# A two-layer decoder trunk on one core: the remainders of the weight pieces are made by an adding transfer instead of a DVE subtraction

## Chip, cores and metric

The kernel runs on 1 core of one Trainium2 chip. The metric is the device time of one execution in microseconds (us). The kernel before takes 2521.07 us, the median of 3 runs (2515.82 to 2522.28).

## What is computed

```
for layer in range(DEPTH):                       # DEPTH = 2, SEQ = 1024, D_MODEL = 1024
    h = rms_norm(x, norm_mix[layer])
    proj = h @ w_in[layer]                       # 1024 x 3584
    q_a, k_a, v_a, q_h, f_h, i_h, g_h = jnp.split(proj, split_points, axis=-1)
    attn = dilated_attention_group(q_a, k_a, v_a, positions)     # 8 heads, 3 strided windows
    attn = rms_norm(attn, attn_out_gain[layer])
    rec = hgrn2_group(q_h, f_h, i_h, g_h, lower_bounds[layer], hgrn_out_gain[layer])
    mixed = jnp.concatenate([attn, rec], axis=-1).astype(x.dtype)
    x = x + mixed @ w_out[layer]                 # 1024 x 1024
    h = rms_norm(x, norm_mlp[layer])
    x = x + jnp.square(jax.nn.relu(h @ w_up[layer])) @ w_down[layer]   # 1024 x 4096 x 1024
return rms_norm(x, norm_final)
```

## The kernel before

Everything stands transposed, features on the 128 partitions and tokens along the free dimension, in two halves of 512 tokens. A float32 product is made of three fast ones: each operand is split into a rounded part (`hi`, type fp32r) and the remainder (`lo` = source - `hi`), and TensorE adds hi·hi, hi·lo and lo·hi into one PSUM bank (`gemm`, lines 376 to 378, and `gemm_tok`, 401 to 403, for products with tokens on the partitions).

Weights come in groups of 128 x 2048. A group is loaded by SP in two halves of 128 x 1024 (512 KB, tag `raw`, 4 buffers). Each half gives two pieces of 128 x 512. `parts` (line 359) makes the pair of one piece in two buffers, `whi` and `wlo` (8 of each): ACT rounds the piece (line 317), DVE subtracts (line 319). `Group.piece` calls it for the weights as loaded. `up_rest` calls it also for s1 to s4, sums and differences of weight pieces: the MLP's first product uses Strassen's scheme with 7 products for 8, of which 3 read pieces as loaded and 4 read s1 to s4. Names of pieces: w0u80l is layer 0, up projection, group 8, piece 0, the remainder. The letters are h (recurrent projections), a (attention projections), o (output projection), u (up), d (down).

A layer runs through: projections and recurrence of the four recurrent heads, attention projections and attention with the first part of the output projection woven in, the norm of the attention output with the rest of the output projection, the MLP's up projection (16 groups), and its down projection. At the very start, the input is scaled, squared and split by ACT and DVE (`norm_in`: `n_0h`, `n_0l`, `n00sq` for the first token half, `n_1h`, `n_1l`, `n01sq` for the second), the squares are summed by two matmuls (`n00ms`, `n01ms`) and the first projection (`psf`, then `psq`) uses the pieces w0h000 to w0h003, then w0h010 to w0h013.

The order of instructions on each engine is not the program's order. Every operation is entered with `op(engine, cost, writes, reads, emit)`, and `Program.order` (line 131) plays the whole program as a list schedule with those costs. Each engine takes the earliest entered operation that is ready and whose buffers are free, at most `LOOKAHEAD` of TensorE work ahead of the oldest one open. A result counts as ready `LATENCY` after its end on another engine, and a buffer as free `RELEASE` after its last reader's end. The order that comes out is then fixed: on the chip each engine goes through its list and waits where an operand isn't there.

Of the kernel before, what the change touches and what calls it, by code (L numbers as in the profile page):

```python
# [11 lines left out]
F32 = mybir.dt.float32  # L12
F32R = mybir.dt.float32r
U32 = mybir.dt.uint32
AF = mybir.ActivationFunctionType
OP = mybir.AluOpType
# [21 lines left out]

COUNT = {"kk": 3, "slot": 64, "raw": 4, "trig": 2, "whi": 8, "wlo": 8, "ls": 4, "last": 2, "row": 2, "rc": 4, "z": 2, "gemm": 3, "sc": 2, "tr": 2, "acc": 1,
         "dram": 1 << 20, "const": 1 << 20}  # L40
LOOKAHEAD = {"PE": 60e3, "SP": 36e3}
PATIENCE = 5e3
RELEASE = {"PE": 200.0, "ACT": 190.0, "DVE": 190.0, "SP": 900.0}
TABLES = {"ln": "natural_log_exp_and_others", "sig": "sigmoid_and_others"}


# [70 lines left out]
class Program:  # L117

    LATENCY = {"PE": 210.0, "ACT": 190.0, "DVE": 190.0, "SP": 1800.0}
    TABLE = 1280.0

    def __init__(self):
# [2 lines left out]
    def op(self, eng, cost, writes, reads, emit, table=None, join=False):  # L127
        engines = eng if isinstance(eng, dict) else {eng: cost}
        self.ops.append(Op(len(self.ops), engines, list(writes), list(reads), emit, table, join))

    def order(self):
        free = dict(COUNT)
        busy = {e: 0.0 for e in self.LATENCY}
        ready = {e: [] for e in self.LATENCY}
        table = "ln"
# [17 lines left out]
        def arrive(o):  # L153
            for e in o.engines:
                heapq.heappush(ready[e], (o.index, o))
# [8 lines left out]
        while done < len(self.ops):  # L164
            while oldest < len(self.ops) and self.ops[oldest].start is not None:
                oldest += 1
            for e in ready:
# [3 lines left out]
                while ready[e]:  # L171
                    item = heapq.heappop(ready[e])
                    o = item[1]
                    if o.start is not None:
                        continue
                    kept.append(item)
                    if oldest < len(self.ops) and ahead[o.index] > ahead[oldest] + LOOKAHEAD.get(e, 60e3):
                        break
# [27 lines left out]
                o = pick  # L206
# [17 lines left out]
            now, _, kind, o = heapq.heappop(events)  # L224
            if kind == "end":
                done += 1
                for b in o.bufs:
                    b.left -= 1
                    if not b.left:
                        seq += 1  # L230
                        heapq.heappush(events, (now + RELEASE[o.on], seq, "free", b))
                for s in o.succs:
                    lag = 0.0 if s.engines.keys() == {o.on} and o.on != "SP" else self.LATENCY[o.on]
                    s.ready = max(s.ready, now + lag)
                    s.waiting -= 1
                    if not s.waiting:
                        seq += 1
                        heapq.heappush(events, (max(now, s.ready), seq, "ready", s))
            elif kind == "free":
                free[o.tag] += 1  # L240
                held[o.tag][oldest:o.last + 1] -= 1
            elif kind == "ready":
                arrive(o)
# [5 lines left out]
def trunk(ctx: ExitStack, tc: tile.TileContext, xT, wts, cols, trig, toep, lmask, ident_d, out):  # L249
    nc = tc.nc  # L250
    V, A, PE = nc.vector, nc.scalar, nc.tensor
# [15 lines left out]
    op = prog.op  # L267
# [26 lines left out]
    def c_act(n):  # L294
        return 80.0 + 0.833 * n

    def c_tt(n):
        return 65.0 + 1.042 * n
# [9 lines left out]
    def whole(b):  # L308
        return b, lambda: b.t
# [5 lines left out]
    def split(hi, lo, src, n=W, join=False):  # L315

        op("ACT", c_act(n), [hi[0]], [src[0]], lambda e: A.copy(hi[1](), src[1]()), join=join)  # L317
        op("DVE", c_tt(n), [lo[0]], [src[0], hi[0]],
           lambda e: V.tensor_tensor(lo[1](), src[1](), hi[1]().bitcast(F32), op=OP.subtract), join=join)  # L319
# [20 lines left out]
    class Group:  # L340
# [13 lines left out]
        def piece(self, i):  # L354
            if i not in self.pieces:
                self.pieces[i] = parts(self.raw(i), f"{self.name}{i}")
            return self.pieces[i]

    def parts(src, name):
        hi, lo = Buf(name + "h", "whi", [128, 512], F32R), Buf(name + "l", "wlo", [128, 512], F32R)  # L360
        split(whole(hi), whole(lo), src, 512)
        return hi, lo

    def gemm(ps, pieces, xs, ts=slice(0, W)):
# [140 lines left out]
    def table():  # L505
        return [[None] * NH for _ in range(KT)]
# [64 lines left out]
    for l in range(L):  # L571
# [628 lines left out]
        hf32, xmid, scale = table(), table(), [None] * NH  # L1200
# [84 lines left out]
        def up_rest(j, grp):  # L1285
            m1 = m1s[j]
            a11, a12, a21, a22 = (grp.raw(i) for i in range(4))
            s1, s2, s3, s4 = (slot(f"s{i}") for i in range(4))
            u2, u3, c12, c22 = (slot(n) for n in ("u2", "u3", "c12", "c22"))
            tt(whole(s1), a21, a22, OP.add)  # L1290
            tt(whole(s2), whole(s1), a11, OP.subtract)
            p = product(parts(whole(s2), "s2"), "t2", "tr")
            tt(whole(u2), whole(m1), p, OP.add)
            tt(whole(s3), a11, a21, OP.subtract)
            p = product(parts(whole(s3), "s3"), "t3", "gemm")
            tt(whole(u3), whole(u2), p, OP.add)
            p = product(parts(whole(s1), "s1"), "t1", "sc")
            tt(whole(c22), whole(u3), p, OP.add)
            relu2(j, 1, 1, c22)
            tt(whole(c12), whole(u2), p, OP.add)  # L1300
            p = product(grp.piece(3), "t4", "tr")
            tt(whole(u3), whole(u3), p, OP.subtract)
            relu2(j, 1, 0, u3)
            tt(whole(s4), a12, whole(s2), OP.subtract)
            p = product(parts(whole(s4), "s4"), "22", "gemm")
            tt(whole(c12), whole(c12), p, OP.add)
            relu2(j, 0, 1, c12)
# [175 lines left out]
```

## Time and profile before

| | us |
|---|---|
| median of 3 runs | 2521.07 (2515.82 to 2522.28) |
| profiled execution, its own time | 2519.49 |
| its span, first to last instruction | 2517.7 |
| TensorE (PE) busy in the span | 2481.2 (99%) |
| weight loads of TensorE (PEld) | 2102.3 (84%) |
| DVE busy | 1685.0 (67%) |
| ACT busy | 966.5 (38%) |
| GpSimd (POOL) busy | 0.2, 4 instructions |
| packets of SP's DMA queue, share of the 16 DMA engines | 37.8%, 314.74 MB |

The profile is of one execution, whose own time lies 1.6 us below the median of the runs. Time outside of the span is 1.8 us. An instruction is named by its line in the kernel, its engine, and its output and inputs. PE's granted clock is 0.995 of full speed over the span. A PE that is busy throughout a stretch is the bound there, whatever the others do; where it is idle, the view of waits names what it waited for.

### The profile page before, as it was taken

How to read it: one execution, taken by the hardware profiler on the slowest of the kernel's cores; microseconds unless marked ns; L12 is line 12 of the kernel's file. 1: busy time of each engine (PE TensorE's matmuls, PEld its weight loads, DVE VectorE, ACT ScalarE, POOL GpSimd, SP SyncE). 2: the span in 40 equal slices, each digit the busy share in tenths (PEclk: the TensorE clock that was granted, in tenths of full speed). 3: DMA queues.
4: the chain of work that ended last, by engine and by line, in shares of the span. 5: the costliest groups of instructions: out<-in, count | busy, mean ns of one | idle time of the engine just before them, and what ended most of it. 6: DMA issues, size and time to landing. Idle time of an engine off the chain costs nothing.

```text
span 2517.7 us, 34893 instructions
## 1 busy us (share of the span) xinstructions
PE 2481.2 (99%) x13004; PEld 2102.3 (84%) x13004; DVE 1685.0 (67%) x3358; ACT 966.5 (38%) x1953; POOL 0.2 (0%) x4
## 2 busy tenths in 40 slices
PE   9999999999999999999999999999999999999998
PEld 7898889787888888888888989898788888888887
DVE  6366868789977675434744678687899777555356
ACT  7233347667322232121432334476662223222123
POOL 0000000000000000000000000000000000000000
PEclk9999999999999999999999999999999999999999
DMA  4011466934333372232220114667344334631311
GB/s 178 19 59 51 151 193 180 274 113 162 128 126 106 127 277 86 73 97 88 88 80 17 60 68 155 194 212 240 110 164 140 124 105 140 236 134 55 105 51 68
DMA packets 140722, 316.98 MB, mean 126 GB/s; under 512 B 17220, under 2 KB 20100, under 8 KB 140552
## 3 DMA queue, kind: packets, MB, share of 16 engines
q1 hardware_dynamic: 140552, 314.74, 37.8%
q8 instruction: 103, 1.69, 0.3%
q14 instruction: 67, 0.55, 0.1%
HBM read 226.36 MB, written 88.32 MB: 125 GB/s over the span
## 4 chain that ended last, share of the span: by engine, by line
PE 92%; DMA 3%; ACT 2%; DVE 2%; SPq 1%; issue 0%; DVEq 0%; ACTq 0%
PE psd L376 9%; PE psd L378 9%; PE psd L377 9%; PE psu L376 8%; PE psu L377 8%; PE psu L378 8%; PE sc L946 2%; PE pa L699 2%; PE pso L377 2%; PE pso L378 2%; PE pso L376 2%; PE pv L1109 2%; PE psva L401 1%; PE psv L401 1%; PE ptr L1096 1%; PE psq L376 1%
## 5 line engine op out<-in xcount | busy, mean ns | idle before, releaser
L306 DVE TENSOR_TENSOR x<-x,psd 128x512 f32<-128x512 f32 x152 | 104.5, 687 | 324.6 <-PE psd L378 323.5
L317 ACT CAST ah<-al 128x512 fp32r<-128x512 f32 x98 | 58.2, 619 | 144.1 <-DVE al L306 140.4
L962 ACT ACTIVATE sp<-sp,ls 128x256 f32<-128x256 f32 (+2 forms) x192 | 100.0, 522 | 21.6 <-DVE ls L951 21.3
L946 PE MATMUL sc<-k,hd 128*128 128x256 f32 (+3 forms) x384 | 94.4, 354 | 11.5 <-DVE ls L951 5.5
L951 DVE CUSTOM_DVE_ANT_0 sp<-sc,tpt 128x256 f32<-128x256 f32 (+1 forms) x192 | 81.6, 439 | 33.9 <-PE sc L946 32.6
L306 DVE TENSOR_TENSOR al<-al,rms 128x512 f32<-128x512 f32 x128 | 81.9, 687 | 4.2 <-DMA al<-a 3.2
L946 PEld LDWEIGHTS sc<-k,hd 128*128 128x128 f32 x384 | 59.6, 191 | 17.8 <-DVE ls L951 7.9
L319 DVE TENSOR_TENSOR al<-al,ah 128x512 fp32r<-128x512 f32 x98 | 64.0, 687 | 4.2 <-ACT ah L317 3.4
L1252 DVE SCALAR_TENSOR_TENSOR c<-c 128x512 f32<-128x512 f32 x96 | 65.9, 686 | 0.0
L319 DVE TENSOR_TENSOR ptl<-ptr,pth 128x512 fp32r<-128x512 f32 (+1 forms) x96 | 60.8, 640 | 6.3 <-ACT pth L317 5.8
L699 PEld LDWEIGHTS pa<-q,k 128*112 128x112 f32 (+3 forms) x512 | 62.0, 184 | 3.3
L306 DVE TENSOR_TENSOR u<-u,psu 128x512 f32<-128x512 f32 x64 | 43.8, 685 | 29.0 <-PE psu L378 28.1
L317 ACT CAST pth<-ptr 128x512 fp32r<-128x512 f32 (+1 forms) x96 | 51.7, 551 | 28.4 <-PE ptr L1096 16.9
L699 PE MATMUL pa<-q,k 128*112 128x64 f32 (+3 forms) x512 | 61.2, 262 | 0.0
L1096 PE MATMUL ptr<-ident,sp 128*128 128x128 f32 x352 | 54.4, 276 | 1.0 <-ACT sp L962 0.9
L306 DVE TENSOR_TENSOR x<-x,pso 128x512 f32<-128x512 f32 x64 | 43.8, 684 | 17.2 <-PE pso L378 16.8
L707 DVE COPY_PREDICATED at<-lmt,pa 126x256 f32<-126x256 uint8 (+1 forms) x64 | 32.6, 510 | 25.9 <-PE pa L699 25.2
L377 PE MATMUL psu<-b22l,s4h 128*128 128x512 f32 x128 | 49.8, 389 | 0.0
L378 PE MATMUL psu<-b22h,s4l 128*128 128x512 f32 x128 | 49.8, 389 | 0.0
L376 PE MATMUL psu<-b22h,s4h 128*128 128x512 f32 x128 | 49.8, 389 | 0.0
L1116 ACT COPY pvt<-pv 64x256 f32<-64x256 f32 x80 | 29.6, 369 | 52.8 <-PE pv L1109 51.7
L376 PE MATMUL psu<-bt2h,s2h 128*128 128x512 f32 x128 | 49.8, 389 | 0.0
(4682 smaller groups left out, 8154.9 us busy)
## 6 DMA issues: line engine op xcount, KB each, us to landing
al<-a SPq DMA_DIRECT2D x128, 256.0 KB
a<-c SPq DMA_DIRECT2D x96, 256.0 KB
w0u<-in_wts_dram SPq DMA_DIRECT2D x40, 512.0 KB
w1u<-in_wts_dram SPq DMA_DIRECT2D x40, 512.0 KB
w0d<-in_wts_dram SPq DMA_DIRECT2D x32, 512.0 KB
w1d<-in_wts_dram SPq DMA_DIRECT2D x32, 512.0 KB
hd<-q SPq DMA_DIRECT2D x48, 256.0 KB
x<-in_x_dram SPq DMA_DIRECT2D x32, 256.0 KB
```

The lines of the kernel that those rows point to most:

```text
L306: lambda e: V.tensor_tensor(dst[1](), a[1](), b[1](), op=kind))
L317: op("ACT", c_act(n), [hi[0]], [src[0]], lambda e: A.copy(hi[1](), src[1]()), join=join)
L319: lambda e: V.tensor_tensor(lo[1](), src[1](), hi[1]().bitcast(F32), op=OP.subtract), join=join)
L376: PE.matmul(ps.t, lhsT=wh[:, cs], rhs=xh[:, ts], start=k == 0, stop=False)
L377: PE.matmul(ps.t, lhsT=wh[:, cs], rhs=xl[:, ts], start=False, stop=False)
L378: PE.matmul(ps.t, lhsT=wl[:, cs], rhs=xh[:, ts], start=False, stop=k == n - 1)
L699: PE.matmul(pa[0:128 - b, c * 64:c * 64 + 64], lhsT=k[:, c * 128:c * 128 + 128 - b], rhs=by_half(q)[:, c, :, 1, :], start=True, stop=True)
L946: PE.matmul(ps[:, o:o + w], lhsT=q[:, q0:q0 + 128], rhs=k[:, keys], start=part == 0, stop=part == 1)
L951: V.tensor_tensor_reduce(t[:, o:o + w], ps[:, o:o + w], tpt[:, x0:x0 + w], -0.125, 3e38, OP.add, OP.min, m.t)
L962: op("ACT", c_act(w) + 190, [t, sum_], [t, m], lambda e, t=t, o=o, w=w, m=m, sum_=sum_: A.activation(t[:, o:o + w], t[:, o:o + w], AF.Exp, ...
L1096: PE.transpose(pt[:, at * 128:at * 128 + 128], t[:, o + kb * 128:o + kb * 128 + 128], ident.t)
L1252: V.scalar_tensor_tensor(t.t, t.t, 0.0, t.t, op0=OP.max, op1=OP.mult)
```

## The change

`parts` no longer calls `split`. ACT rounds the piece as before and then writes the negative of the rounded part into the remainder's buffer. GpSimd's queue issues a transfer from SBUF to SBUF that adds the source to that buffer: the remainder is -`hi` + source. The planner gets GpSimd as a fifth engine with figures of its own. `split` itself stays, for the activations.

```
-LOOKAHEAD = {"PE": 60e3, "SP": 36e3}
+LOOKAHEAD = {"PE": 60e3, "SP": 36e3, "POOL": 36e3}
-RELEASE = {"PE": 200.0, "ACT": 190.0, "DVE": 190.0, "SP": 900.0}
+RELEASE = {"PE": 200.0, "ACT": 190.0, "DVE": 190.0, "SP": 900.0, "POOL": 2500.0}
+DMA = ("SP", "POOL")
...
-    LATENCY = {"PE": 210.0, "ACT": 190.0, "DVE": 190.0, "SP": 1800.0}
+    LATENCY = {"PE": 210.0, "ACT": 190.0, "DVE": 190.0, "SP": 1800.0, "POOL": 4000.0}
...
-                    lag = 0.0 if s.engines.keys() == {o.on} and o.on != "SP" else self.LATENCY[o.on]
+                    lag = 0.0 if s.engines.keys() == {o.on} and o.on not in DMA else self.LATENCY[o.on]
...
     def parts(src, name):
         hi, lo = Buf(name + "h", "whi", [128, 512], F32R), Buf(name + "l", "wlo", [128, 512], F32R)
-        split(whole(hi), whole(lo), src, 512)
+        op("ACT", c_act(512), [hi], [src[0]], lambda e: A.copy(hi.t, src[1]()))
+        op("ACT", c_act(512), [lo], [hi], lambda e: A.activation(lo.t, hi.t.bitcast(F32), AF.Copy, scale=-1.0))
+
+        op("POOL", 1300.0, [lo], [src[0]], lambda e: nc.gpsimd.dma_start(lo.t.bitcast(F32), src[1](), accum_op=OP.add))
         return hi, lo
```

Lines behind the diff's place move by 1 to 4: the rounding of a weight piece is line 362, the negation 363, the adding transfer 365, and the products 380 to 382.

**ACT's queue at the start.** Before, the part of the list that ends the rounding of the first three pieces (n_0 and n_1 are the two token halves, x_0 and x_1 their loads):

```order
L317 CAST w0h000h<-w0h_91 128x512
L317 CAST w0h001h<-w0h_91 128x512
L323 ACTIVATE n_0h<-x_0_93,colt 128x512
L323 ACTIVATE n_0h<-x_0_97,colt 128x512
L313 ACTIVATE n00sq<-x_0_93 128x512
L323 ACTIVATE n_0h<-x_0_103,colt 128x512
L313 ACTIVATE n00sq<-x_0_97 128x512
L313 ACTIVATE n00sq<-x_0_103 128x512
L317 CAST w0h002h<-w0h_107 128x512
```

And with the change, at the same place and at the end of the squares of the second half:

```order
L362 CAST w0h000h<-w0h_91 128x512
L362 CAST w0h001h<-w0h_91 128x512
...
L314 ACTIVATE n00sq<-x_0_103 128x512
L363 ACTIVATE w0h000l<-w0h000h 128x512
...
L363 ACTIVATE w0h001l<-w0h001h 128x512
L362 CAST w0h002h<-w0h_107 128x512
...
L314 ACTIVATE n01sq<-x_1_223 128x512
L363 ACTIVATE w0h002l<-w0h002h 128x512
L362 CAST w0h003h<-w0h_107 128x512
L362 CAST w0h010h<-w0h_149 128x512
```

The negation of the first piece now stands where the rounding of the third stood, and that of the third piece stands behind all eight squares of the second token half; the roundings of w0h003 and w0h010, which stood ahead of those squares, stand behind it.

**TensorE's queue where the output projection begins** (pso, in layer 0's attention; sc, ptr and pv are the scores, transposes and products with the values). Before:

```order
L946 MATMUL sc<-k,hd 128x256 x2
L946 MATMUL sc<-k,hd 128x512 x2
L1096 MATMUL ptr<-ident,sp 128x128 x3
L376 MATMUL pso<-mh,w0o100h 128x512
L377 MATMUL pso<-mh,w0o100h 128x512
L378 MATMUL pso<-mh,w0o100l 128x512
```

And with the change:

```order
L950 MATMUL sc<-k,hd 128x256 x2
L1100 MATMUL ptr<-ident,sp 128x128 x4
L950 MATMUL sc<-k,hd 128x256 x4
L1100 MATMUL ptr<-ident,sp 128x128 x3
L1113 MATMUL pv<-pth,vv 128x256
L1113 MATMUL pv<-ptl,vv 128x256
L1113 MATMUL pv<-pth,vv 128x128
L1113 MATMUL pv<-ptl,vv 128x128
L380 MATMUL pso<-mh,w0o100h 128x512
L381 MATMUL pso<-mh,w0o100h 128x512
L382 MATMUL pso<-mh,w0o100l 128x512
```

More attention work now stands ahead of the first product with w0o100.

## Rows read from the trace of the kernel before

**Rows 1.** The page's first part: busy time of each engine, its share, instructions.

```profile
PE 2481.2 (99%) x13004; PEld 2102.3 (84%) x13004; DVE 1685.0 (67%) x3358; ACT 966.5 (38%) x1953; POOL 0.2 (0%) x4
```

**Rows 2.** Stretches of 60 us: each engine's busy us, clock, DMA share, GB/s.

```profile
0.00:60.00 60.00, 56.80 (x254) 46.02 (x255) 40.79 (x76) 46.07 (x77) 0.20 (x4) 0.97 0.50 180
...
420.00:480.00 60.00, 56.04 (x385) 49.44 (x383) 45.12 (x129) 37.12 (x108) 0.00 (x0) 1.00 0.82 251
...
540.00:600.00 60.00, 55.79 (x242) 45.12 (x241) 49.89 (x84) 40.92 (x75) 0.00 (x0) 0.94 0.29 98
...
720.00:780.00 60.00, 60.00 (x266) 49.54 (x265) 45.46 (x74) 14.68 (x24) 0.00 (x0) 1.00 0.33 110
...
2460.00:2520.00 60.00, 49.06 (x304) 43.45 (x302) 34.29 (x66) 21.49 (x48) 0.00 (x0) 0.93 0.20 71
```

**Rows 3.** Waits of PE over the span: us in total, times, longest us.

```profile
PE sc L946 <- DVE ls L951: 5.5, 6, 2.1
PE sc L946 <- DMA k<-kl: 4.0, 5, 1.9
...
PE pso L377 <- DVE ma_0l L319: 2.6, 2, 1.3
PE sc L946 <- DMA hd<-q: 1.8, 2, 1.1
PE pso L377 <- DVE ma_1l L319: 1.6, 2, 0.8
...
PE pso L378 <- DVE w1o100l L319: 1.0, 1, 1.0
```

**Rows 4.** Four remainders, by tile: instructions, ns min/median/max, first and last start.

```profile
L378 PE MATMUL psu<-b,w0u90l x3: 392/398/398, 774.5 to 777.2; 128*128 128x512 f32 x3
L319 DVE TENSOR_TENSOR w0u90l<-w0u,w0u90h x1: 690/690/690, 757.5 to 757.5; 128x512 fp32r<-128x512 f32 x1
...
L378 PE MATMUL psd<-a,w0d1610l x3: 392/398/398, 1107.2 to 1108.6; 128*128 128x512 f32 x3
L319 DVE TENSOR_TENSOR w0d1610l<-w0d,w0d1610h x1: 685/685/685, 1076.8 to 1076.8; 128x512 fp32r<-128x512 f32 x1
...
L378 PE MATMUL pso<-mh,w0o100l x8: 389/391/497, 453.9 to 509.3; 128*128 128x512 f32 x8
L319 DVE TENSOR_TENSOR w0o100l<-w0o,w0o100h x1: 693/693/693, 453.1 to 453.1; 128x512 fp32r<-128x512 f32 x1
```

**Rows 5.** ACT in order of time, first 30 us: start, us, instruction.

```profile
11.12 0.60 ACT L317 CAST w0h002h<-w0h 128x512 fp32r<-128x512 f32 x1
...
16.18 0.60 ACT L317 CAST w0h003h<-w0h 128x512 fp32r<-128x512 f32 x1
16.69 0.62 ACT L317 CAST w0h010h<-w0h 128x512 fp32r<-128x512 f32 x1
...
27.39 0.62 ACT L313 ACTIVATE n01sq<-x 128x512 f32<-128x512 f32 x1
```

**Rows 6.** PE in order of time, first third product: start, us, instruction.

```profile
6.95 0.49 PE L378 MATMUL psf<-n_0h,w0h000l 128*128 128x512 f32 x1
```

**Rows 7.** The first 34.5 us, instructions of psf alone, then of psq alone.

```profile
0.00:34.50 34.50, 23.93 (x90) 17.35 (x90) 1.38 (x2) 0.95 0.65 236
0.00:34.50 34.50, 2.18 (x9) 1.88 (x10) 0.00 (x0) 0.95 0.65 236
```

**Rows 8.** Transfers on the chain that ended last: start, us, what.

```profile
345.32 6.92 DMA mh<-mhh
...
462.69 3.11 DMA l<-mw
```

**Rows 9.** Line 319's subtractions of s1; ACT's most frequent rounding, with mean ns.

```profile
L319 DVE TENSOR_TENSOR s1l<-s,s1h x32: 684/686/696, 641.7 to 2130.8; 128x512 fp32r<-128x512 f32 x32
...
L317 ACT CAST ah<-al 128x512 fp32r<-128x512 f32 x98 | 58.2, 619 | 144.1 <-DVE al L306 140.4
```

## The prediction

> **What bounds the kernel now.** I read the busy times first, then the stretches, then what TensorE waits for, then single remainders. TensorE is busy 2481.2 of 2517.7 us and DVE 1685.0 [rows 1]. The stretches [rows 2] show that this is no average over unlike stages: in the MLP (720 to 780 us) TensorE has no idle time at all and issues 266 matmuls in 60 us, 0.226 us each, at full clock. There DVE has 14.5 us and ACT 45.3 us free in 60. So nothing that DVE is spared in such a stretch can shorten it. TensorE's idle time, 36.5 us in all, sits elsewhere: 3.2 us in the first 60 us, 4.0 at 420 to 480 us (attention), 4.2 at 540 to 600 us (the norm behind it), similar amounts at the same places in layer 1, and 8.6 us in the last stretch, which ends at 2517.7, behind the last weights. In the waits [rows 3] the part that DVE ends is small: 5.5 us for score blocks, 2.6 and 1.6 for remainders of activations, 1.0 for a remainder of a weight piece. Two waits of 4.0 and 1.8 us are ended by transfers.
>
> How far ahead of its use is a remainder made? [Rows 4]: w0u90l in the up projection is ready at 758.2 us (757.5 + 0.69) and first used at 774.5, 16.3 us later; w0d1610l in the down projection 29.7 us before its use. But w0o100l, where the output projection begins inside attention, is used at 453.9, just as it is ready. So there are two kinds of places: deep ones, where a later remainder costs nothing, and shallow ones, the start of the program and of the output projection.
>
> **The change part by part.** It removes 496 DVE subtractions (7 pieces in each of 32 up groups, 272 others) of 0.686 us each [rows 9]: 340 us of DVE. It adds 496 negations on ACT, which I take at the 0.62 us of a rounding of the same size [rows 9]: 307 us, for an ACT that has 967 of 2518 [rows 1]. And it adds 496 transfers of 256 KB on GpSimd's queue, which was empty, so that only these transfers queue behind one another there.
>
> *What one adding transfer takes from its issue to its landing.* No row shows one. The nearest rows are transfers on the chain: 3.11 us for one of 8 KB and 6.92 us for one of 256 KB under load [rows 8]. I keep both as ends and take the middle, 5.0 us, since DMA is about two thirds busy at the start, between the two. The Trainium skill ("DMA: Bandwidth & Descriptors", section "Anatomy of one DMA") gives 2.0 us plus bytes over 436 GB/s for a transfer issued by GpSimd; as an estimate from that page this is 2.6 us for 256 KB, and by it the start below would cost 9.0 instead of 9.9 us. No row of this trace shows a GpSimd transfer.
>
> *The deep places* (recurrent and attention projections, up, down). The path from rounding to remainder grows from one subtraction (0.69) to a negation and a transfer, 0.62 + 5.0 us, so by 4.9 us (3.0 to 6.9). Against 16.3 and 29.7 us of lead [rows 4] this costs nothing. The cover is the ring of 8 remainder buffers, and it is gone if the transfers cannot keep the pace (rivals below).
>
> *The start.* This is my largest term, and it comes from the order of ACT's list rather than from the transfer. Before, the third product runs at 6.95 us [rows 6], and the rounding of w0h002 at 11.12 us [rows 5]. With the change the first negation stands where that rounding stood, so it ends at about 11.7 us and the first remainder lands at 14.8 to 18.6 us: TensorE stands at its third product. That alone would be made up partly, but the negation of w0h002 stands behind the eighth square of the second half. Before, that square ends at 28.0 us [rows 5]. Up to it ACT's list has gained two negations and lost two roundings (w0h003 and w0h010, which stood at 16.2 and 16.7 us), so it is reached at the same time: 28.0, the negation ends at 28.7 with one short copy between, and the remainder lands at 33.7 us (31.8 to 35.6). Until then TensorE can do no more than the two pieces before it, 48 products, and two of w0h002. Before, 99 products of psf and psq had been done by 34.5 us [rows 7], so about 96 by 33.7. TensorE is 46 products behind, 10.4 us at 0.226, less the two matmuls of the second sum (0.5 us) that it has already done: 9.9 us, from 9.0 (where the second sum itself, not before 32.8 us, becomes the limit) to 11.7. Since TensorE is idle nowhere soon after this, the loss stays.
>
> *The output projection inside attention.* The path to w0o100l is 4.9 us longer, but the planner has put two more score pairs, seven transposes and four products ahead of its first use. I take no net cost, and 0 to 4.9 us for each layer as the range.
>
> *DVE's relief.* It can only show where TensorE waits for DVE: at most the 10.7 us of the four DVE rows [rows 3]. Of the instructions queued ahead of those results few are subtractions of weight pieces, some 28 per layer in attention and norm. I take 2 us, with 0 to 10.7 as bounds.
>
> *Transfers in attention.* The DMA engines are 82% busy at 420 to 480 us [rows 2], where score loads are already waited for, 5.8 us in all [rows 3]. Adding transfers there delay loads; I take 2 us, 0 to 5.8.
>
> The sum is 9.9 + 0 - 2 + 2 = 9.9 us on the execution's own 2519.5 us: 2529.4, rounded 2530. Against the median of 2521.07 us that is +0.35%, just above 0.3% (2513.5 to 2528.6 us), which is about what a measurement of this kernel can tell from no change. With the ends (start 9.0 to 11.7, relief 10.7 at most, transfers 5.8, output projection) this case spans 2518 to 2547 us.
>
> **The rivals.** *The DMA engines become the bound in the up projection.* An up group is 84 products, 18.95 us, with 7 adding transfers. The other traffic takes 33% of the engines there at 110 GB/s [rows 2], so full use would be about 333 GB/s and a copy of 256 KB takes 0.79 us of all 16 engines. The remaining 67%, 12.7 us, allows 1.81 us for each adding transfer. As ends, it costs one copy (0.79) or, if both reads and the write each count as one, three (2.36); I take two (1.57), nearest to a transfer that reads twice what it writes. Two fit, with 91% used; three don't: 7 x 2.36 + 6.3 = 22.8 us for a group, 3.8 us more, 123 us over 32 groups. At 2.0 us each it is 1.3 us more for a group, 42 us in all, 2572 us. For it: how near 91% is to full. Against: buffers hold 16 us of lead, and in the down projection pieces are fewer. The Trainium skill ("Collectives: The Full Stack", section "The bandwidth ceiling: the fold count and why AG ≠ RS ≠ AR") says that an add in the transfer path halves the rate because two sources are read; by that page it would be two copies, so this rival would not happen. No transfer of this kind is in the trace.
>
> *GpSimd's issue becomes the bound.* If it needs more than 18.95 / 7 = 2.71 us for each, the up groups stretch: at 3.0 us by 2.1 us each, 66 us, 2596 us. SP issues a transfer in 0.3 to 0.4 us, which speaks against it; but GpSimd's only rows are four fills at the start [rows 1], so nothing shows its price.
>
> *The other side: DVE's relief pays for the start.* Place: attention and the norms, where the queue in front of the awaited DVE results gets shorter by subtractions of 0.69 us. It decides if it brings over 9.9 us; the four rows hold 10.7, so with nearly all of it, and chains through ACT shortened beside it, the time is 2519 us, no change; with a start limited less than I reckon, 2512. For it: DVE is busy 45 and 50 us of 60 there [rows 2]. Against: most of what is queued there is attention work.
>
> *The change does not move the work*: if the negation and transfer ended as early as the subtraction, the time would be 2519.5. The listed order of ACT speaks against it.
>
> **How the numbers follow.** Forecast 0.52, of which two thirds lie above 2528.6. DMA bound 0.18, GpSimd bound 0.06, relief pays 0.20 (0.08 of it below 2513.5), nothing moves 0.04. Slower: 0.34 + 0.18 + 0.06 = 0.58; faster 0.08; same 0.18 + 0.12 + 0.04 = 0.34. The range is 2515 to 2580 us: it takes in the forecast's own 2518 to 2547, the relief case except its best part, and the DMA case up to about 2.05 us for each transfer, and leaves out some 0.2.
>
> **What would show it.** Right: the third psf product starts at 15 to 19 us instead of 6.95; the first product with w0h002l at 32 to 36 us; by 34.5 us about 50 products of psf; DVE about 340 us less busy, ACT about 307 more; no idle TensorE in the up groups; the DMA engines below 95% there. Wrong: TensorE waiting in the up projection on s1l to s4l or w0u remainders (one of the two bounds; GpSimd's spans and the DMA share tell which), or a start that loses under 5 us, or waits on scores and norms that are gone.

## The result, and the profile after

The change makes the kernel slower: 2596.68 us median (2593.45 to 2599.75, 4 runs) against 2519.55 us (2515.82 to 2522.28, 4 runs), a ratio of 1.0307 (95% interval 1.0288 to 1.0326). The prediction had the sign, but its 2530 us and its range up to 2580 us are too low. The profiled execution took 2596.29 us, its span is 2594.5 us; that of the kernel before was 2517.7, so 76.8 us are to be found.

The page of the kernel after, engines and DMA queues (packets, MB, share of 16 engines; q0 is GpSimd's queue, q1 SP's):

```profile
PE 2502.4 (96%) x13004; PEld 2114.1 (81%) x13004; DVE 1402.5 (54%) x2867; ACT 1234.0 (48%) x2440; POOL 430.3 (17%) x500
...
q1 hardware_dynamic: 140552, 314.74, 36.7%
q0 software_dynamic: 71424, 130.06, 29.0%
```

Against [rows 1], DVE lost 282.5 us and ACT gained 267.5, so the work moved as meant. But TensorE's idle time went from 36.5 to 92.1 us, and its busy time, for the same 13004 products, rose by 21.2 us. Both together are the 76.8 us. ACT's gain and DVE's loss are smaller than the 307 and 340 us foreseen. Rows of consecutive instructions overlap, which would explain it: the rounding at 16.18 us lasts 0.60 us, and the next starts at 16.69 [rows 5].

Stretches of the kernel after (columns as in [rows 2]):

```profile
0.00:60.00 60.00, 44.31 (x189) 35.78 (x190) 28.98 (x55) 46.38 (x80) 10.80 (x16) 0.89 0.79 223
...
660.00:720.00 60.00, 56.00 (x239) 45.18 (x240) 34.35 (x55) 30.29 (x52) 18.96 (x22) 0.99 0.93 220
720.00:780.00 60.00, 60.00 (x263) 49.54 (x262) 35.81 (x57) 27.63 (x44) 19.00 (x22) 0.99 0.93 223
780.00:840.00 60.00, 60.00 (x265) 49.49 (x264) 29.85 (x46) 28.55 (x47) 18.97 (x22) 1.00 0.92 216
1740.00:1800.00 60.00, 52.25 (x294) 43.61 (x292) 36.30 (x103) 39.22 (x110) 6.92 (x8) 0.91 0.99 277
```

From 720 to 840 us, in the middle of the up projection, TensorE has no idle time although the DMA engines are 92 and 93% busy (0.33 before [rows 2]). The losses lie around such stretches, not in them: in the first 60 us, where the up projection begins (660 to 720), and in attention of layer 1, where the DMA share is 0.99.

What TensorE waits for in the kernel after (total us, times, longest):

```profile
PE sc L950 <- DMA k<-kl: 15.9, 9, 3.2
PE psf L382 <- DMA w0h000l<-w0h: 11.6, 1, 11.6
PE psd L380 <- ACT ah L318: 8.1, 2, 5.0
...
PE psa L382 <- DMA w1a110l<-w1a: 3.2, 1, 3.2
PE psu L382 <- DMA s3l<-s: 3.1, 2, 1.8
PE psu L380 <- DVE u L307: 3.0, 2, 1.9
...
PE psa L382 <- DMA w0a110l<-w0a: 2.4, 1, 2.4
...
PE pso L382 <- DMA w0o110l<-w0o: 2.1, 1, 2.1
...
PE pso L382 <- DMA w1o110l<-w1o: 1.4, 1, 1.4
...
PE rc L478 <- ACT n01rs L314: 1.1, 1, 1.1
...
PE n01ms L431 <- ACT n01sh L318: 1.0, 1, 1.0
```

The wait of score blocks for reloaded keys (k<-kl), 4.0 us before [rows 3], is the longest; then come the first remainder, and a rounded activation at the begin of the down projection (psd for ah), which was no wait before. TensorE also waits for late remainders themselves: 9.1 us for four pieces of attention's input and output projections (a and o), and 3.1 us for s3l, 1.8 at the begin of up in layer 0 and 1.3 in layer 1.

To find all the places, the first use of a stage's first weight piece was read from both traces, and the difference taken stage by stage (begin of up ends at the first use of w0u43, a piece of its fifth group). The same was done for the runs below. All numbers are us later than before, per stage:

| stage (ends at, before) | the change | order, DVE adds | thin transfers | transfers in MLP | transfers in attention | in deep places | same, not the last up groups |
|---|---|---|---|---|---|---|---|
| start, recurrent heads (226.4) | 11.7 | 11.7 | 11.3 | 0.1 | -0.3 | -0.2 | -0.3 |
| attention, norm, layer 0 (601.4) | 13.3 | 6.6 | 6.6 | -0.8 | 17.7 | 4.8 | -3.2 |
| begin of up, layer 0 (708.6) | 7.1 | 0.2 | 0.0 | 1.3 | 0.0 | 0.0 | 0.0 |
| rest of up, first down block (997.2) | 8.4 | 0.6 | -0.2 | 10.4 | -0.2 | 6.5 | -0.3 |
| rest of down, recurrent heads, layer 1 (1476.2) | 0.0 | 0.0 | 0.0 | 0.0 | 0.0 | 0.0 | 0.0 |
| attention, norm, layer 1 (1846.8) | 21.9 | 9.6 | 8.6 | 2.9 | 21.0 | -2.1 | 1.2 |
| begin of up, layer 1 (1954.0) | 3.8 | 0.0 | 0.0 | 2.8 | 0.0 | 0.0 | 0.0 |
| rest of up, first down block (2242.3) | 10.1 | 1.5 | 0.0 | 11.2 | 0.0 | 7.8 | 0.0 |
| end (2517.7) | 0.5 | 0.0 | 0.5 | 0.1 | 0.1 | 0.1 | 0.1 |

The change's column falls into three parts: start 11.7, attention 35.2, the MLP's edges 29.4. Attention's rows also hold what any new plan scatters: in runs that leave its pieces to DVE they lie between -3.2 and +4.8.

**The start** in the kernel after: psf alone up to 34.5 us (columns as in [rows 7]), then rows of two first remainders and of the second sum of squares by tile.

```profile
0.00:34.50 34.50, 13.95 (x51) 10.49 (x52) 0.68 (x1) 0.80 0.74 235
```
```profile
L382 PE MATMUL psf<-n_0h,w0h000l x4: 400/628/797, 18.7 to 22.4; 128*128 128x512 f32 x4
...
L365 POOL DMA_DIRECT2D w0h000l<-w0h x1: 1004/1004/1004, 11.5 to 11.5; - x1
...
L382 PE MATMUL psf<-n_0h,w0h002l x4: 393/397/398, 34.5 to 38.3; 128*128 128x512 f32 x4
...
L363 ACT ACTIVATE w0h002l<-w0h002h x1: 622/622/622, 29.3 to 29.3; 128x512 fp32r<-128x512 f32 x1
L365 POOL DMA_DIRECT2D w0h002l<-w0h x1: 862/862/862, 30.2 to 30.2; - x1
...
DMA to landing us min/median/max: 3.7/3.7/3.7
...
L431 PE MATMUL n01ms<-n01sh,ones_r x1: 494/494/494, 33.0 to 33.0; 128*128 128x512 f32 x1
```

TensorE stands until w0h000l is used at 18.7 us, and reaches w0h002l at 34.5 with 51 products of psf done, against 99 of psf and psq before [rows 7]. It doesn't wait for w0h002l there: that remainder lands at 33.9, while the second sum of squares, which stands ahead of it in TensorE's list, could begin only at 33.0, behind a wait for ACT's n01sh.

**The begin of the down projection** in the kernel after, on the chain that ended last (start, us, what):

```profile
934.03 6.76 DMA al<-a
...
941.54 0.63 ACT ah L318
...
944.52 6.36 DMA w0d<-in_wts_dram
...
951.49 0.62 ACT ah L318
952.15 0.80 PE psd L380
...
953.67 0.43 PE psd L382
```

One of the microseconds behind the wait (columns as in [rows 2]):

```profile
953.00:954.00 1.00, 1.00 (x3) 0.81 (x4) 1.00 (x3) 1.00 (x3) 0.79 (x1) 0.50 0.07 29
```

The activation that TensorE needs is rounded only at 951.49, because ACT stands for a weight load that SP issued at 944.52. Behind the wait a product adds 0.43 us to the chain (the first 0.80), where products add 0.23 us in steady work: the granted clock is 0.50 there, TensorE at 1.2 GHz in place of 2.4, after it has stood for 5.0 us. The granted clock is 0.89 in the first 60 us (0.97 before, [rows 2]) and 0.91 from 1740 to 1800. Of the 21.2 us of added busy time some 11 lie in attention and 10.5 at the begins of up and down; the start, with the longest wait, has none (0.8 us less than before). How much of it is the clock was not measured apart.

### The profile page after: what moved, and what is told of

Read it like the earlier page. It is cut to its first block, busy times and chain, and to the rows that moved or that the text cites. A ratio compares the mean times of both kernels' runs of the same rounds, so it can differ in the third digit from the quotient of the medians.

```text
span 2594.5 us, 36485 instructions
## 1 busy us (share of the span) xinstructions
PE 2502.4 (96%) x13004; PEld 2114.1 (81%) x13004; DVE 1402.5 (54%) x2867; ACT 1234.0 (48%) x2440; POOL 430.3 (17%) x500
## 3 DMA queue, kind: packets, MB, share of 16 engines
q1 hardware_dynamic: 140552, 314.74, 36.7%
## 4 chain that ended last, share of the span: by engine, by line
PE 80%; DMA 12%; DVE 3%; ACT 2%; issue 2%; SPq 1%; DVEq 0%; POOL 0%; ACTq 0%; POOLq 0%
PE psd L380 9%; PE psd L381 9%; PE psd L382 9%; PE psu L380 5%; PE psu L381 5%; PE psu L382 5%; PE sc L950 2%; PE pa L703 2%; DMA k<-kl 2%; PE pv L1113 2%; PE pso L382 1%; PE pso L381 1%; PE pso L380 1%; PE psv L405 1%; PE ptr L1100 1%
## 5 line engine op out<-in xcount | busy, mean ns | idle before, releaser
L950 PE MATMUL sc<-k,hd 128*128 128x256 f32 (+3 forms) x384 | 100.0, 364 | 17.9 <-DMA k<-kl 15.9
L307 DVE TENSOR_TENSOR al<-al,rms 128x512 f32<-128x512 f32 x128 | 82.3, 685 | 22.9 <-DMA al<-a 14.3
L1120 ACT COPY pvt<-pv 64x256 f32<-64x256 f32 x80 | 29.6, 370 | 67.5 <-PE pv L1113 66.3
L382 PE MATMUL psu<-bt3h,s3l 128*128 128x512 f32 x128 | 50.0, 391 | 3.1 <-DMA s3l<-s 3.1
L380 PE MATMUL psu<-bt1h,s1h 128*128 128x512 f32 x128 | 49.9, 390 | 1.0 <-DVE c L307 1.0
```

The lines of the kernel that those rows point to most:

```text
L307: lambda e: V.tensor_tensor(dst[1](), a[1](), b[1](), op=kind))
L380: PE.matmul(ps.t, lhsT=wh[:, cs], rhs=xh[:, ts], start=k == 0, stop=False)
L382: PE.matmul(ps.t, lhsT=wl[:, cs], rhs=xh[:, ts], start=False, stop=k == n - 1)
L950: PE.matmul(ps[:, o:o + w], lhsT=q[:, q0:q0 + 128], rhs=k[:, keys], start=part == 0, stop=part == 1)
```

## The experiments

The first question is how much of the loss is transfer and how much is order. By theory A the adding transfers make it, through the time that they take of the DMA engines and until they land, beside the negations at the start; by theory B the new order of the planner makes it, which knows GpSimd by 1.3 us for an issue, 4 us until the result is there and 2.5 us until a buffer is free.

**The change's order, with no transfer.** The sum stands where the planner put the transfer, but DVE makes it.

```
-        op("POOL", 1300.0, [lo], [src[0]], lambda e: nc.gpsimd.dma_start(lo.t.bitcast(F32), src[1](), accum_op=OP.add))
+        op("POOL", 1300.0, [lo], [src[0]], lambda e: V.tensor_tensor(lo.t, src[1](), lo.t.bitcast(F32), op=OP.add))
```

> The planned order, the negations on ACT and all buffers are those of the change; only the adding itself is done by DVE, at the place in the whole order where the change issues its transfer. Theory A (transfers land late, and crowd the DMA engines): the losses in attention and at the two ends of the up projection go, what stays is most of the start, whose limit is the place of the third negation in ACT's list: 2526 to 2533 us. Theory B (the re-planned lists are to blame, whoever adds): 2580 us or more.

Measured: 2550.37 us, ratio 1.0124 (1.0109 to 1.0139), 33 us above the kernel before in its series, and so between the two theories: the MLP's losses go as A said, but attention keeps 16.2 us that A had given to the transfers. Order and negations alone cost two fifths of the loss: the whole start, 16.2 us of attention, and only 2.3 us in the MLP. Waits of TensorE in this run, and rows of the third piece's remainder by tile:

```profile
PE sc L950 <- DMA k<-kl: 9.4, 9, 2.1
PE psf L382 <- DVE w0h000l L365: 6.0, 1, 6.0
```
```profile
L382 PE MATMUL psf<-n_0h,w0h002l x4: 389/393/397, 34.5 to 38.2; 128*128 128x512 f32 x4
...
L365 DVE TENSOR_TENSOR w0h002l<-w0h,w0h002l x1: 685/685/685, 30.3 to 30.3; 128x512 fp32r<-128x512 f32 x1
```

Here w0h002l is ready at 31.0 us, 2.9 us sooner than in the change, and TensorE still uses it at 34.5; the wait for the first remainder is 6.0 for 11.6 us, and the start's loss is still 11.7. So neither remainder sets that loss. What both runs share is the second sum of squares, ahead of w0h002l in TensorE's list: it begins at 32.9 us here and at 33.0 in the change.

**The transfers, in the order of the kernel before.** At the place of each DVE subtraction stand an ACT negation and the adding transfer.

```
-        split(whole(hi), whole(lo), src, 512)
+        op("ACT", c_act(512), [hi], [src[0]], lambda e: A.copy(hi.t, src[1]()))
+
+        def emit(e):
+            A.activation(lo.t, hi.t.bitcast(F32), AF.Copy, scale=-1.0)
+            nc.gpsimd.dma_start(lo.t.bitcast(F32), src[1](), accum_op=OP.add)
+
+        op("DVE", c_tt(512), [lo], [src[0], hi], emit)
```

> The planned order of the kernel before; at each place where DVE subtracted, ACT negates and GpSimd issues the adding transfer. Theory A: the same transfers, the same late landings and crowding, 2570 us or more; the start loses some 4 us instead of 12 since the negations come early. Theory B: 2520 to 2535 us, because the order of before is kept.

Measured: 2663.91 us, ratio 1.0570 (1.0550 to 1.0590). With the transfers in, the planner's new order is 67 us better than the old one, though it costs 33 us by itself. Theory B, that the order alone makes the loss, falls. The start loses 13.1 us, not the 4 expected: the first remainder is waited for 8.9 us.

**Thin transfers.** Same instructions and order; a transfer adds 128 of 512 columns. In the other columns the remainder stays the negative rounded part, so part of the computation is left out.

```
-        op("POOL", 1300.0, [lo], [src[0]], lambda e: nc.gpsimd.dma_start(lo.t.bitcast(F32), src[1](), accum_op=OP.add))
+        op("POOL", 1300.0, [lo], [src[0]],
+           lambda e: nc.gpsimd.dma_start(lo.t[:, 0:128].bitcast(F32), src[1]()[:, 0:128], accum_op=OP.add))
```

> The order of the change with all its transfers, but each adds only 128 of the 512 columns (rows of 512 bytes for 2 KB), so the remainders of the other columns are left as the negative rounded part. Number of transfers, packets and GpSimd issue stay. If crowding of the DMA engines is what makes the landings late, the losses in attention and MLP go and the start stays: 2530 to 2550 us. If the fixed part of a landing (3.2 us for the fastest in the trace) or the order is to blame: 2580 us or more.

Measured: 2544.69 us, ratio 1.0099 (1.0082 to 1.0116), 52 us below the change. Stage by stage it reads like the run in which DVE adds. Its DMA queue and the longest waits of TensorE:

```profile
q0 software_dynamic: 71424, 32.54, 11.1%
```
```profile
PE sc L951 <- DMA k<-kl: 11.0, 9, 2.2
PE psf L383 <- DMA w0h000l<-w0h: 10.2, 1, 10.2
```

With a quarter of the bytes, the same 496 issues and negations cost nothing in the MLP, and no more than the order in attention. So GpSimd's issue isn't the bound, and what the transfers cost beyond the order comes with their bytes. These act in two ways that this run doesn't part: the queue's share of the DMA engines falls from 29.0 to 11.1%, and the landings get shorter too (s2l 3.8 us in the median for 6.2).

**The first pieces split by DVE** (names w0h0...), the rest as in the change.

```
+        if name.startswith("w0h0"):
+            split(whole(hi), whole(lo), src, 512)
+            return hi, lo
```

> As the change, but the pieces of the first four groups (w0h000 to w0h033) are split by DVE as before. The start's share is 12 of the 77 us by the stages of the two traces: 2583 to 2587 us if it is a separate loss; nearer to 2597 if the time lost at the start would have been lost later anyway.

Measured: 2586.26 us, ratio 1.0269 (1.0254 to 1.0284), 10.4 us below the change. The start's share is separate; the later stages together keep their losses (66.3 us in the profile, 65.1 in the change).

**Negation and DVE sum, planned as DVE work.** The kernel before with one more ACT instruction for each piece; no GpSimd in the plan.

```
-        split(whole(hi), whole(lo), src, 512)
+        op("ACT", c_act(512), [hi], [src[0]], lambda e: A.copy(hi.t, src[1]()))
+        op("ACT", c_act(512), [lo], [hi], lambda e: A.activation(lo.t, hi.t.bitcast(F32), AF.Copy, scale=-1.0))
+        op("DVE", c_tt(512), [lo], [src[0]], lambda e: V.tensor_tensor(lo.t, src[1](), lo.t.bitcast(F32), op=OP.add))
```

> The kernel before with the change's arithmetic (ACT copy, ACT negation, then a sum) but the sum on DVE and planned as a DVE operation with DVE's own times. ACT has the 496 negations more (496 x 0.619 = 307 us), DVE as before. Theory A (the 33 us that the change's order costs without any transfer come from the plan's times for GpSimd, 4 us of latency and 2.5 us until a buffer is free): about before plus the negations of the first pieces, 2518 to 2528 us. Rival N (the negations themselves, as work in ACT's list ahead of what TensorE waits for): 2540 to 2552 us, as the run with DVE additions in the change's order.

Measured: 2533.36 us, ratio 1.0060 (1.0043 to 1.0077): between the two. In its profile 6.3 us are lost at the start and 3.6 in attention, nothing in the MLP; the profiled execution, 2529.17 us, is the fastest of four, so the stages show 9.7 of the median's 14.8 us. So with the negations in ACT's list and no GpSimd in the plan about half of the start's 11.7 us comes about; the other half needs the order planned around GpSimd.

**Transfers in the MLP only, and in attention only.**

```
+        if name[2:3] in ("h", "a", "o"):
+            split(whole(hi), whole(lo), src, 512)
+            return hi, lo
```
```
+        if name[2:3] not in ("a", "o"):
+            split(whole(hi), whole(lo), src, 512)
+            return hi, lo
```

> Adding transfers in the up and down products (352 of 496); the pieces of the q/k/v input, attention and output projections are split by DVE. Theory A: what remains is the begin of up and of down, in the change +7.2 and +8.4 us in layer 0 and +5.0 and +8.9 in layer 1, together 29.5; with the start and attention gone 2540 to 2550 us. Rival: the late begin of up is itself a consequence of attention's lateness, then its 12 go too: 2530 to 2538.

> Adding transfers only for the q/k/v and output projections (40 of 248 a layer). Theory A: attention loses what it lost in the change, 13 us in layer 0 and 22 in layer 1, and nothing else does: 2548 to 2558 us. Rival O (attention loses by the plan's order alone, as in the run with DVE additions in the change's order, 7 and 10 us): 2530 to 2538 us. Rival L (attention lost because it was late already from the start): 2518 to 2524 us.

Measured: MLP only 2546.61 us, ratio 1.0108 (1.0093 to 1.0123); attention only 2555.89 us, ratio 1.0145 (1.0127 to 1.0163). The parts add up: 38.7 us of attention here, 25.7 at the MLP's edges there, 11.7 at the start of the change are 76.1 of 76.8. That this fits so well is partly luck: attention loses 3.5 us more than in the change, the begin of down 3.1 more, the begin of up 6.8 less. In the MLP-only run the begin of up lost 4.1 us instead of 10.9: there the rival was partly right, more than half of that loss needs the transfers ahead of it, or the order planned with them. Those of attention alone don't make it either (0.0 in both layers).

**Attention's order, with no transfer.** The attention-only run, in which DVE makes the 80 sums at the places planned for GpSimd.

```
-        op("POOL", 1300.0, [lo], [src[0]], lambda e: nc.gpsimd.dma_start(lo.t.bitcast(F32), src[1](), accum_op=OP.add))
+        op("POOL", 1300.0, [lo], [src[0]], lambda e: V.tensor_tensor(lo.t, src[1](), lo.t.bitcast(F32), op=OP.add))
```

> The run with transfers in attention only, in the same planned order, but each of its 80 sums is made by DVE on the remainder's buffer and no adding transfer runs. That run lost 17.7 us in attention of layer 0 and 21.0 in layer 1. Theory A (order about 16 us, as in the whole change's order with DVE additions, and the transfers' bytes the other 20 or so): 2530 to 2538 us. Rival O (all of it is order): 2550 to 2558 us. Rival T (all of it is the transfers): 2517 to 2524 us.

Measured: 2534.58 us, ratio 1.0067 (1.0044 to 1.0090); in its stages 8.0 and 8.5 us. So attention's 38.7 us are 16.5 of order, with the negations in it, and 22.2 of transfers; any new plan scatters by some 3 to 5 us in a layer, so neither number is sharper than that. Of the run's 16.6 us above the span before, 8.6 are longer busy time of TensorE and 8.0 idle time (2489.8 of 2534.3 us busy, against [rows 1]), at a mean granted clock of 0.991 for 0.995. The largest single wait grows by 9.5 us with the transfers; here it is first with them, then without:

```profile
PE sc L953 <- DMA k<-kl: 18.1, 10, 3.5
```
```profile
PE sc L953 <- DMA k<-kl: 8.6, 9, 2.0
```

Another 8.6 us are waits for the remainders w0a110l, w1a110l, w0o110l and w1o110l, which only the run with transfers has.

**Transfers in the deep places only.** Fourth pieces and sums from the fifth up group on, first and second pieces from the ninth, down pieces from the second block; all others are split by DVE.

```
-    def parts(src, name):
+    def parts(src, name, deep=False):
...
+        deep = deep or name[2:3] == "d" and name[3] != "0" or name[2:3] == "u" and int(name[3:-1]) >= (4 if name[-1] == "3" else 8)
+        if not deep:
+            split(whole(hi), whole(lo), src, 512)
+            return hi, lo
...
-            p = product(parts(whole(s2), "s2"), "t2", "tr")
+            p = product(parts(whole(s2), "s2", j >= 4), "t2", "tr")
...
```

> Adding transfers only where the piece is made long before its use: from the fifth group of the up phase on (sums and fourth pieces; first and second pieces from the ninth group) and the down products from the second block of 8 on. That is 124 of 248 transfers of a layer; all other pieces are split by DVE as before. Theory A (bytes and order hurt only at narrow places: start, attention, begin of up, begin of down): 2516 to 2523 us, no loss, and no gain either although DVE is rid of 248 subtractions. One bound: if the crowding at the begin of down moves to the second block, up to 9 us a layer more, 2535. Theory D (every transfer costs alike: the 46 us between the change and the run with DVE additions in the change's order, over 496 transfers, 93 ns each): 248 x 0.093 = 23 us, 2541.

Measured: 2534.13 us, ratio 1.0063 (1.0048 to 1.0078): neither number. The loss isn't spread over the transfers: 14.3 us of it sit at the begin of down, whose own first block is split by DVE. The chain of this run shows why (start, us, what):

```profile
888.13 8.48 DMA s1l<-s
896.60 0.02 SPq L339
...
896.66 4.79 DMA al<-a
```

SP reads an activation of the up projection back (al) only at 896.66, as soon as the transfer that reads the buffer of s1 has landed, 8.48 us after its issue. So the reading back for the next phase waits for transfers of the last up groups, and shares the DMA engines with them.

**The same, without the last four up groups.**

```
-        deep = deep or name[2:3] == "d" and name[3] != "0" or name[2:3] == "u" and int(name[3:-1]) >= (4 if name[-1] == "3" else 8)
+        deep = deep or name[2:3] == "d" and name[3] != "0" or name[2:3] == "u" and (4 if name[-1] == "3" else 8) <= int(name[3:-1]) < 12
...
-            p = product(parts(whole(s2), "s2", j >= 4), "t2", "tr")
+            p = product(parts(whole(s2), "s2", 4 <= j < 12), "t2", "tr")
...
```

> As the run with transfers in the deep places only, but the last four up groups of each layer are split by DVE again (96 transfers a layer in place of 124). There the begin of down lost 6.5 and 7.5 us although its own first block was split by DVE, and the share of the DMA engines in the last up groups was 0.90 to 1.05 against 0.32 to 0.71 before, just where the activations for down are read back. Theory A2 (the last up groups' transfers hold up that reading back): the begin of down loses nothing, 2516 to 2525 us, with up to 5 us of order scattered in attention of layer 0. Rival O (the plan's order for the begin of down, with GpSimd's times in it): the loss stays, 2530 to 2536 us.

Measured: 2519.71 us, ratio 1.0007 (0.9994 to 1.0021), and the begin of down loses nothing. Stretches around it, of the kernel before, of the run with all deep places, and of this one:

```profile
840.00:900.00 60.00, 60.00 (x266) 49.44 (x265) 47.37 (x77) 20.61 (x35) 0.00 (x0) 1.00 0.48 157
900.00:960.00 60.00, 60.00 (x263) 49.00 (x262) 29.48 (x48) 11.92 (x20) 0.00 (x0) 1.00 0.62 221
```
```profile
840.00:900.00 60.00, 60.00 (x265) 49.44 (x264) 27.19 (x42) 27.68 (x46) 17.26 (x20) 1.00 0.96 228
900.00:960.00 60.00, 54.96 (x235) 43.51 (x234) 38.07 (x62) 16.36 (x29) 0.00 (x0) 1.00 0.74 259
```
```profile
840.00:900.00 60.00, 60.00 (x265) 49.45 (x265) 48.01 (x78) 20.61 (x35) 0.00 (x0) 1.00 0.51 168
900.00:960.00 60.00, 60.00 (x265) 49.35 (x264) 27.89 (x46) 11.30 (x19) 0.00 (x0) 1.00 0.56 198
```

With the DMA engines at 0.96 in the last up groups TensorE loses 5 us in the next 60; at 0.51 it loses none. A high share alone isn't the loss: in the kernel before the engines are 0.97 busy from 920 to 940 us, with the loads for down, and TensorE has no idle time. What differs is when these loads come: in the kernel before SP issues 15 reloads of al from 875 to 901 us, with all deep places 9 from 875 to 906. This run also plans the last groups without GpSimd, but the order has little to do with it: the run with DVE additions in the change's order lost 0.6 and 1.5 us at the begin of down. And the 192 transfers of this run take 112 us of busy time off DVE (1572.9 left of 1685.0 [rows 1]), which buys nothing.

**A plan with the measured times**: 0.862 us for an issue, 6 us to landing, 5 us until a buffer is free.

```
-RELEASE = {"PE": 200.0, "ACT": 190.0, "DVE": 190.0, "SP": 900.0, "POOL": 2500.0}
+RELEASE = {"PE": 200.0, "ACT": 190.0, "DVE": 190.0, "SP": 900.0, "POOL": 5000.0}
...
-    LATENCY = {"PE": 210.0, "ACT": 190.0, "DVE": 190.0, "SP": 1800.0, "POOL": 4000.0}
+    LATENCY = {"PE": 210.0, "ACT": 190.0, "DVE": 190.0, "SP": 1800.0, "POOL": 6000.0}
...
-        op("POOL", 1300.0, [lo], [src[0]], lambda e: nc.gpsimd.dma_start(lo.t.bitcast(F32), src[1](), accum_op=OP.add))
+        op("POOL", 862.0, [lo], [src[0]], lambda e: nc.gpsimd.dma_start(lo.t.bitcast(F32), src[1](), accum_op=OP.add))
```

> The change with the planner told what the change's trace shows: 0.862 us for an issue instead of 1.3, 6 us from issue to use instead of 4, and 5 us until the raw buffer is free instead of 2.5. Theory A (the narrow places lack room and transfer time, no order gives it back): 2580 to 2620 us, since a longer latency in the plan also sets more of the order by it. Rival C (the change loses because the plan's times are too short): at most 2560 us.

Measured: 2598.04 us, ratio 1.0316 (1.0293 to 1.0339), as the change. In its stages the begin of up is cured (0.8 and 0.0 us), but attention loses 51.6 us instead of 35.2: a plan that lengthens every remainder makes attention worse; how much of that is order and how much transfers is open.

**Only the pieces before the norm**, the one stage where the change gained time.

```
+        if name[2:4] != "o0":
+            split(whole(hi), whole(lo), src, 512)
+            return hi, lo
```

> Adding transfers for the second half of the output projection alone (8 of 248 a layer), the one stage in which the change was faster than before, by 2.5 and 1.5 us. Theory G (DVE's relief shortens the norm between output projection and up): 2513 to 2516 us, faster than both. Rival B (the stage only gave back a lateness that the stage before it had made): 2517 to 2524 us.

Measured: 2517.49 us, ratio 0.9995 (0.9982 to 1.0008): no change. The stage gains 4.4 us in each layer, and the one before it, up to the first of these pieces, loses 4.1 and 5.0. It gives back a lateness and earns nothing. No run here beats the kernel before.

## Why the prediction was wrong

- **What bounds the kernel** held: TensorE in the MLP, with no gain for a freer DVE.
- **The start** held in its numbers: the third product at 18.7 us (15 to 19 foreseen), w0h002l at 34.5 (32 to 36), 51 products by 34.5 us (about 50). The loss is 11.7 us for a forecast of 9.9, at the range's upper end. That it comes from order and negations and not from the transfer is shown: with DVE sums in the same order it is 11.7 as well. But the limit that the middle value was reckoned from, the landing of w0h002l, is not the one: TensorE stands behind the second sum of squares, which the prediction named only for its lower end of 9.0. It came at 33.0 us (32.8 foreseen), and the next step on its result (rc) is waited for another 1.1 us. That both limits lie within a microsecond of each other made the number come out.
- **The landing** was estimated at 5.0 us (3.1 to 6.9). Medians of the kernel after, per tile (issues, KB each, us to landing):

```profile
s2l<-s POOLq DMA_DIRECT2D x32, 256.0 KB, 6.2
...
s4l<-s POOLq DMA_DIRECT2D x32, 256.0 KB, 4.2
```

  Then all 496 together, from the view of line 365:

```profile
DMA to landing us min/median/max: 3.2/4.7/11.2
```

  The middle was right, the upper end was not: the four remainders of attention that TensorE waited for took 7.7 to 9.6 us, the first one of all 7.1. The Trainium skill ("DMA: Bandwidth & Descriptors", section "Anatomy of one DMA") gives a sum by which, as an estimate from that page, 2.6 us would come for this size; these two medians are 1.6 and 2.4 times that, so the measurement decides.
- **The DMA engines as the bound in up** (the rival) did not come, though the sign set for it, TensorE waiting on s1l to s4l in up, did appear with 3.1 us at the two begins of up; behind the first groups there is none. Its middle value, two copies or 1.57 us of all engines for a transfer, was right. From the page, 29.0% of 2594.5 us over 496 transfers is 1.52 us. The Trainium skill ("Collectives: The Full Stack", section "The bandwidth ceiling: the fold count and why AG ≠ RS ≠ AR") has an add read two sources and so halve the rate; the trace agrees with the factor, since a copy on q1 takes 0.79 us for 256 KB (36.7% of 2594.5 us, over 314.74 MB), and doesn't show the reason.
- **GpSimd's issue as the bound** did not come: 0.862 us for an issue, where 2.71 would have decided.
- **"The deep places ... this costs nothing" failed at the phases' edges.** The lead was read from two pieces in the middle, and there it holds. At the begin of up the lead before was much shorter: s3l was ready at 644.3 us and used at 649.3, 5.0 us for the 16.3 taken (start, us, instruction, kernel before):

```profile
643.63 0.68 DVE L319 TENSOR_TENSOR s3l<-s,s3h 128x512 fp32r<-128x512 f32 x1
```
```profile
649.26 0.39 PE L378 MATMUL psu<-bt3h,s3l 128*128 128x512 f32 x1
```

  An adding transfer also reads and so holds the buffer of its source until it lands: ACT and DVE waited 29.7 us in all for landings on line 365 before they could write other results (ah 12.6, c 8.7, s 8.4). And the transfers fill the DMA engines to 0.9. Where the up projection begins and where its results are read back for down, the next phase needs just these: 29.4 us, for a forecast of 0. How the 29.4 divide between the held buffers and the engines' time isn't shown. Attention's input projections, also counted as deep, cost 5.6 us of waits for w0a110l and w1a110l.
- **"The output projection inside attention" and "Transfers in attention"**, together 2 us with at most 15.6 as the ends, failed in size: 35.2 us. The second had the right mechanism (late score loads, k<-kl from 4.0 to 15.9 us in TensorE's waits), but it was bounded by the waits that existed before, and a wait that grows isn't bounded by its old length. The first took the planner's new order as free of cost; the attention-only pair shows 16.5 us of order and 22.2 of transfers. The late remainders of the output projection were sized rightly: 2.1 and 1.4 us of waits, for 0 to 4.9 in each layer.
- **DVE's relief**, 2 us: none is seen. The gain at the norm is a lateness given back, and the run with 192 transfers is level with the kernel before.

What stays open: why the planner's order in attention costs those 16.5 us. No run took apart which of the moved instructions does it, nor what part the negations have: where they were planned as such, without GpSimd, attention lost 3.6 us.

## What to carry to other kernels

Moving work from an engine with free time to the DMA engines bought nothing here and spent two copies of transfer time for each sum; look for who else needs these engines at the phase's edges, not only at its middle. A lead of buffers measured in the middle of a phase says nothing of its first and last groups, where a transfer that lands late also holds the buffer that the next phase's loads want. When a planner is told of a slower operation, count the new order itself as a cost: a run that keeps the order and makes the operation in the old way measures it.

## What was not expected of the hardware

- The DMA engines were 92 to 93% busy from 720 to 840 us with TensorE at no idle time.
- GpSimd's row for an adding transfer shows 0.862 us, its landing comes 3.2 to 11.2 us after the issue. The Trainium skill ("Perfetto Trace Analysis", section "DMA Instruction — SWDGE (GPSIMD)") says that such a row ends when the descriptors are made, not when the data has moved; the trace agrees.
- Taking a DVE subtraction of 0.686 us [rows 9] away freed 0.57 us of busy time (282.5 over 496), and a negation of 0.62 us added 0.54 (267.5 over 496).
- A wait can cost more than its length: behind the 5.0 us at the begin of down the products follow at 0.43 us, granted clock 0.50, where steady ones follow at 0.23. The change as a whole added 55.6 us of idle and 21.2 us of busy time.
